# A transformer layer on one core: store queue, x tiles, operand order, buffer places and pool starts

## The chip, the cores and the metric

One core of a Trainium2 chip runs the kernel. The metric is device time in microseconds, the median of the runs shown. Engines: TensorE (PE, with weight loads as PEld), VectorE (DVE), ScalarE (ACT), GpSimd (POOL) and SyncE (SP), which issues most DMAs. SP, and ScalarE where it issues DMAs, take their instructions in order: an issue that waits holds up everything behind it on that engine.

## The reference

One layer on x of 2048 tokens by 1024 channels, float32, with a conditioning vector c:

```python
h = rms_norm(x, g_attn[l]) * (1.0 + scale_a) + shift_a
proj = h @ w_in[l]                      # q, k, v of 8 FoX heads and 8 stick-breaking heads, forget logits
mix = jnp.concatenate([head_rms_norm(o_fox, ...), head_rms_norm(o_sb, ...)], axis=-1)
x = x + gate_a * (mix @ w_out[l])
h = rms_norm(x, g_mlp[l]) * (1.0 + scale_m) + shift_m
u = causal_depthwise_conv(h @ w_up[l], conv_w[l], conv_b[l])     # 2 x 2752 columns, width 3
u_gate, u_val = jnp.split(u, 2, axis=-1)
x = x + gate_m * ((jax.nn.silu(u_gate) * u_val) @ w_down[l])
return rms_norm(x, g_final)
```

## The kernel before

Every matrix product keeps float32 accuracy by splitting each operand into a high part (fp32r) and the rest: `split` (L43 to L45) lets ScalarE write the high part and DVE or POOL subtract. Three matmuls (high·high, high·low, low·high) stand for one product.

The stages in order are the input projection with attention (to about 1.6 ms), the output projection, the up projection and the down projection.

**Output projection** (L623 to L738). Eight units `u` of 256 tokens. `make_mix` loads the attention output o and its scales r and splits the product into mix tiles, one unit ahead. `out_proj` takes two x1 tiles (`x1_tile`, L722: three buffers), loads x into each (L627, SP), computes 2 x 24 matmuls per tile (L632) and adds the result on DVE (L636); L637 stores the sum on SP. `finish_out` (L708) then scales the rows, transposes the two tiles on TensorE (L716), applies the modulation on ScalarE into hf_m tiles (L718, three buffers) and stores each to DRAM as h (L720, SP), 64 stores in all. An x1 tile is free again once the transposes of its unit are done.

**Up projection** (L741 to L926). Two half sequences `sblk` of 1024 tokens, each with 21 pairs of 128-column blocks and a rest of 64 columns. A Strassen-like scheme uses seven products over four index steps j instead of eight. `h_operands` loads two tiles xh of h per j and makes the operands: `oa` (the four blocks themselves, b12 replaced by b12 − b11) and `ob` (three differences), each split into two. j = 0's oa and ob lie in pool `hop0`, those of j = 1 to 3 in `hop1`. `w_operands` does the like with weight blocks (`ws`, `wu` in pool `wup`). The first pair of a half (`pair_first`, L823) runs all seven products of j = 0, then of j = 1, and so on, so that it can begin before all h is there; the other pairs (`pair`) run one product over all j. The first half needs only the tokens of units 0 to 3, so its work overlaps the end of the output projection. Then follow convolution (L871 to L881), SiLU, and a store of the product to DRAM as g (L903; L925 for the rest of 64).

**Down projection** (L928 to L999). For each of four blocks of 512 tokens, 22 steps k load a graw tile (L943) and a wdraw tile (L934), split both (`g` on ScalarE and POOL, `wd` on ScalarE and DVE, six buffers each) and run 24 matmuls (L966) into eight banks; L958 and L959 load gm and gf for the tail, where the residual add, the norm and two stores (L999, one on SP, one on ScalarE) follow.

**Pools.** SBUF is a stack from the left and one from the right. The constants lie at the bottom of the left one; `open_pool` opens a pool on either side, and a tile waits for the readers of the tiles whose bytes it takes. `hop0` and `wup` are on the right, `p2a`, `p2b`, `hop1`, `up` and `down` on the left. Left pools begin at byte 5440 and on, a multiple of 64; the right ones' tiles start 32 bytes off such a multiple. In the down projection, as it is before, every tile takes bytes of `hop1` and `up`.

The order of instructions on each engine is set when the program is built: the tile framework schedules them by a simulated timeline within the order that data and buffers leave free.

Of the kernel before, what the change touches and what calls it, by code (L numbers as in the profile page):

```python
# [16 lines left out]
P = 128  # L17
S = 2048
D = 1024
# [14 lines left out]
def kernel(ctx: ExitStack, tc: tile.TileContext, x, c, w_ada, b_ada, g_attn, w_in, b_fgate,  # L34
# [5 lines left out]
    def f(t):  # L40
        return t.bitcast(F32)
# [40 lines left out]
    epsc = const.tile([P, 1], F32, name="epsc")  # L82
    nc.vector.memset(epsc, EPS)

    cols = const.tile([P, P], F32, name="cols")
    conv = const.tile([P, 4, 2 * NFULL + 1], F32, name="conv")
    cs = const.tile([P, KT], F32, name="cs")
    mod_a = const.tile([P, 2, KT], F32, name="mod_a")
# [619 lines left out]
    def finish_out(u, xts):  # L708
        sl = slice(u % 4 * HT, (u % 4 + 1) * HT)
        r = rms_scale(p2b, xts, "m")  # L710
        for i, xt in enumerate(xts):
            nc.vector.tensor_scalar_mul(xt, xt, r[:, i:i + 1])
        for kt in range(KT):
            ps = bank(psd, "t", 2)
            for i, xt in enumerate(xts):
                nc.tensor.transpose(ps[:, i * P:(i + 1) * P], xt[:, kt * P:(kt + 1) * P], ident)  # L716
            hf = p2b.tile([P, HT], F32, name="hf_m", bufs=3)
            nc.scalar.activation(hf, ps[:, :HT], AF.Identity, scale=mod_m[:, 0, kt:kt + 1],  # L718
                                 bias=mod_m[:, 1, kt:kt + 1])
            nc.sync.dma_start(hms[u // 4][kt][:, sl], hf)  # L720

    def x1_tile():  # L722
        return p2b.tile([P, D], F32, name="x1", bufs=3)

    mixes = {}
    for u in range(NU):
# [26 lines left out]
    def h_operands(sblk, j):  # L753

        pool = ho if j == 0 else ho1
        xh = ho.tile([P, 2, SB], F32, name="xh", bufs=2)
        for i in range(2):
            nc.sync.dma_start(xh[:, i], hms[sblk][j + i * NK])
        b = pool.tile([P, 3, 2, TB], F32R, name=f"ob{j}")
        a = pool.tile([P, 4, 2, TB], F32R, name=f"oa{j}")  # L760
        tt = ho.tile([P, 2, TB], F32, name="tt", bufs=1)
        b11, b12 = xh[:, 0, 0:TB], xh[:, 0, TB:SB]
        b21, b22 = xh[:, 1, 0:TB], xh[:, 1, TB:SB]

        def put(hi, lo, s):
            split(hi, lo, s, nc.vector)

        put(a[:, 0, 0], a[:, 0, 1], b11)
        put(a[:, 1:3, 0], a[:, 1:3, 1], xh[:, 1].rearrange("p (a n) -> p a n", n=TB))
        nc.gpsimd.tensor_sub(tt[:, 0], b22, b12)  # L770
        nc.gpsimd.tensor_sub(b12, b12, b11)
        put(a[:, 3, 0], a[:, 3, 1], b12)
        nc.vector.tensor_sub(tt[:, 1], b22, b12)
        put(b[:, 0:2, 0], b[:, 0:2, 1], tt)
        nc.gpsimd.tensor_sub(b21, b21, tt[:, 1])
        put(b[:, 2, 0], b[:, 2, 1], b21)
        return [a[:, 0], b[:, 1], a[:, 1], a[:, 3], b[:, 0], a[:, 2], b[:, 2]], a

    def load_up(col_sets):
# [12 lines left out]
    def w_operands(ci):  # L792

        g, v = load_up([(ci * P, P)]), load_up([(DFF + ci * P, P)])
        a11, a12, a21, a22 = g[:, 0:NK], g[:, NK:KT], v[:, 0:NK], v[:, NK:KT]
        s3 = wp.tile([P, NK, P], F32, name="ws", bufs=4)
        s2 = wp.tile([P, NK, P], F32, name="ws", bufs=4)
        nc.gpsimd.tensor_sub(s3, a11, a21)
        nc.gpsimd.tensor_add(a21, a21, a22)
        nc.gpsimd.tensor_sub(s2, a21, a11)  # L800
        yield w_split(a11)
        yield w_split(s2)
        yield w_split(a12)
        nc.gpsimd.tensor_sub(a12, a12, s2)
        yield w_split(a21)
        yield w_split(s3)
        yield w_split(a12)
        yield w_split(a22)

    def product(b, w, o, j, first, last):  # L810
        for i, (p, q) in enumerate(((0, 0), (0, 1), (1, 0))):
            nc.tensor.matmul(b, w[:, p, j], o[:, q], start=first and i == 0, stop=last and i == 2,  # L812
                             skip_group_check=True)
# [9 lines left out]
    def pair_first(ws, yg, yv):  # L823

        banks = [bank(psd, "o", 4), bank(psd, "o", 4), bank(psd, "o", 4), bank(psd, "o", 4),
                 bank(psd, "t", 2), bank(psd, "t", 2), bank(psc, "bc", 2)]
        for j in range(NK):
            for b, w, o in zip(banks, ws, obs[j][0]):
                product(b, w, o, j, j == 0, j == NK - 1)
        b1, b6, b2, b5, b7, b3, b4 = banks  # L830
        p1, t, u3 = snap(), snap(), snap()
        nc.scalar.activation(p1, b1, AF.Copy)
        nc.vector.tensor_add(t, b6, p1)
        nc.vector.tensor_add(yg[:, T0], b2, p1)
        nc.vector.tensor_add(u3, b7, t)
        nc.vector.tensor_add(t, b5, t)
        nc.vector.tensor_add(yv[:, T1], b5, u3)
        nc.vector.tensor_add(yg[:, T1], b3, t)
        nc.vector.tensor_add(yv[:, T0], b4, u3)
# [85 lines left out]
        nc.sync.dma_start(gs[NFULL][sblk], sg[REST:P])  # L925
    close_pool("up", "hop1", "wup", "hop0")  # L926

    dp = open_pool("down")  # L928

    def load_down(k):  # L930
        n = P if k < NFULL else REST
        raw = dp.tile([P, D], F32, name="wdraw", bufs=3)
        for r in range(P // n):
            nc.sync.dma_start(raw[r * n:(r + 1) * n], w_down[k * P:k * P + n, :])  # L934
        w = dp.tile([P, 2, D], F32R, name="wd", bufs=6)
        split(w[:, 0], w[:, 1], raw, nc.vector)
        return w

    def load_g(k, tb):
        n = P if k < NFULL else REST  # L940
        raw = dp.tile([P, TB], F32, name="graw", bufs=3)
        for r in range(P // n):
            nc.sync.dma_start(raw[r * n:(r + 1) * n], gs[k][tb // 2][:, tb % 2 * TB:(tb % 2 + 1) * TB])  # L943
        g = dp.tile([P, 2, TB], F32R, name="g", bufs=6)
        if n == P:
            split(g[:, 0], g[:, 1], raw)
        else:
            nc.scalar.activation(g[:, 0], raw, AF.Copy)
            nc.vector.tensor_sub(g[REST:P, 0], raw[REST:P], f(g[REST:P, 0]))
        return g  # L950

    gm = dp.tile([P, D], F32, name="gm")
    gf = dp.tile([P, D], F32, name="gf")
    LAST = 4
    NKD = NFULL + 1
    for tb in range(NTB):
        if tb == 0:
            nc.sync.dma_start(gm, gate_m)  # L958
            nc.sync.dma_start(gf, g_final.rearrange("(o n) -> o n", o=1).to_broadcast([P, D]))  # L959
        banks = [[bank(psd, "o", 4) for _ in range(2)] for _ in range(2)]  # L960
        banks += [[bank(psd, "t", 2) for _ in range(2)], [bank(psc, "bc", 2) for _ in range(2)]]

        def step(k, g, w, t, n):
            seq = ((0, 0), (0, 1), (1, 0)) if k < NFULL else ((0, 0), (0, 1))
            for i, (a, b) in enumerate(seq):
                nc.tensor.matmul(banks[t][n], g[:, a, t * P:(t + 1) * P], w[:, b, n * TB:(n + 1) * TB],  # L966
                                 start=k == 0 and i == 0, stop=k == NKD - 1 and i == len(seq) - 1)

        tail = []
        for k in range(NKD):  # L970
            g, w = load_g(k, tb), load_down(k)
            if k >= NKD - LAST:
                tail.append((k, g, w))
                continue
            for t in range(4):
                for n in range(2):
                    step(k, g, w, t, n)
        for t in range(4):
            row = tb * 4 + t
            xt = dp.tile([P, D], F32, name="xo", bufs=4)  # L980
            nc.sync.dma_start(xt, x1s[row])
            ss = dp.tile([P, 2], F32, name="sl_f", bufs=4)
            r = dp.tile([P, 1], F32, name="r_f", bufs=4)
            for n in range(2):
                sl = slice(n * TB, (n + 1) * TB)
                for k, g, w in tail:
                    step(k, g, w, t, n)
                y = dp.tile([P, TB], F32, name="yo", bufs=3)
                nc.vector.tensor_mul(y, banks[t][n], gm[:, sl])
                nc.vector.tensor_add(xt[:, sl], xt[:, sl], y)  # L990
                junk = dp.tile([P, TB], BF16, name="junk_f", bufs=2)
                nc.scalar.activation(junk, xt[:, sl], AF.Square, accum_out=ss[:, n:n + 1])
            nc.vector.tensor_add(r, ss[:, 0:1], ss[:, 1:2])
            nc.scalar.activation(r, r, AF.Sqrt, bias=epsc, scale=1.0 / D)
            nc.vector.reciprocal(r, r)
            for n, q in enumerate((nc.sync, nc.scalar)):
                sl = slice(n * TB, (n + 1) * TB)
                nc.vector.scalar_tensor_tensor(xt[:, sl], xt[:, sl], r, gf[:, sl], ALU.mult, ALU.mult)
                q.dma_start(out[row * P:(row + 1) * P, sl], xt[:, sl])  # L999

    close_pool("down", "psd", "psc")

# [22 lines left out]
```

## Time and profile before

| | |
|---|---|
| median of 3 runs | 3206.13 us (3205.09 to 3209.88) |
| profiled execution | 3209.97 us, span 3207.9 us |
| TensorE busy | 3018.6 us, 94% of the span |
| DVE / ACT / POOL busy | 2178.5 / 1657.6 / 1230.3 us |
| output projection, units 1 to 7 | about 1641.8 to 1824 us |
| its end, with the first pair of the up projection | to 1870.5 us |
| change of half sequences | 2257.9 to 2301.3 us |
| last up matmul, first down matmul | 2708.95 us, 2726.28 us |

Times in views count from the start of the span. "PE ps_o L632 <- DVE x L636" says that the matmul of line 632, which writes tile ps_o, waited for DVE's instruction of line 636 on tile x. PEclk is the granted TensorE clock in parts of 2.4 GHz. A chain's "issue" is time in which an engine waited for nothing that is shown.

### The profile page before, as it was taken

How to read it: one execution, taken by the hardware profiler on the slowest of the kernel's cores; microseconds unless marked ns; L12 is line 12 of the kernel's file. 1: busy time of each engine (PE TensorE's matmuls, PEld its weight loads, DVE VectorE, ACT ScalarE, POOL GpSimd, SP SyncE). 2: the span in 40 equal slices, each digit the busy share in tenths (PEclk: the TensorE clock that was granted, in tenths of full speed). 3: DMA queues.
4: the chain of work that ended last, by engine and by line, in shares of the span. 5: the costliest groups of instructions: out<-in, count | busy, mean ns of one | idle time of the engine just before them, and what ended most of it. 6: DMA issues, size and time to landing. Idle time of an engine off the chain costs nothing. (4 is left out here: it accounts for less than half of the span.)

```text
span 3207.9 us, 46681 instructions
## 1 busy us (share of the span) xinstructions
PE 3018.6 (94%) x16190; PEld 2526.4 (79%) x16190; DVE 2178.5 (68%) x3335; ACT 1657.6 (52%) x3033; POOL 1230.3 (38%) x1399
## 2 busy tenths in 40 slices
PE   7899898999899999999988899999899997999999
PEld 5778787878778888888866678888688886888887
DVE  6787888978867765557733477777887786354353
ACT  5666676656656665566633344444544443333332
POOL 2554455656542232240132234444544442322221
PEclk8999999999999999999998899999999999999999
DMA  8547542556355876593466332222232222664652
GB/s 262 177 153 255 149 142 53 169 187 180 105 171 167 278 245 200 177 331 100 164 201 214 138 103 83 82 82 80 76 92 83 82 79 78 221 200 149 199 200 86
DMA packets 292940, 496.53 MB, mean 155 GB/s; under 512 B 29448, under 2 KB 177664, under 8 KB 291680
## 3 DMA queue, kind: packets, MB, share of 16 engines
q1 hardware_dynamic: 290288, 489.32, 47.7%
q10 hardware_dynamic: 2416, 4.23, 0.3%
q8 instruction: 128, 2.10, 0.3%
q14 instruction: 108, 0.88, 0.1%
HBM read 352.61 MB, written 90.51 MB: 138 GB/s over the span
## 5 line engine op out<-in xcount | busy, mean ns | idle before, releaser
L812 PE MATMUL ps_o<-oa,wu 128*128 128x512 f32 x2088 | 514.2, 397 | 7.1 <-ACT oa L44 3.9
L812 PEld LDWEIGHTS ps_o<-oa,wu 128*128 128x128 f32 x2088 | 392.9, 189 | 105.9 <-ACT oa L44 5.3
L405 PE MATMUL ps_pv<-at,V 128*128 128x256 f32 x2304 | 412.1, 297 | 32.5 <-DVE at L401 19.5
L401 DVE TENSOR_TENSOR at<-ps_pt,at 128x512 fp32r<-128x512 f32 (+1 forms) x576 | 363.4, 651 | 111.1 <-ACT at L400 108.4
L287 PE MATMUL ps_pj<-hp,w_qk 128*128 128x512 f32 x1512 | 417.0, 407 | 11.2 <-POOL hp L45 3.4
L400 ACT ACTIVATE at<-ps_pt 128x512 fp32r<-128x512 f32 (+1 forms) x576 | 315.7, 577 | 215.3 <-PE ps_pt L396 173.8
L426 DVE TENSOR_TENSOR_SCAN r<-r 128x513 f32<-128x513 f32 (+2 forms) x320 | 383.6, 1213 | 38.6 <-ACT r L419 29.2
L427 POOL TENSOR_TENSOR a<-a,r 128x512 f32<-128x512 f32 (+3 forms) x240 | 280.4, 1171 | 308.3 <-DVE r L426 178.9
L405 PEld LDWEIGHTS ps_pv<-at,V 128*128 128x128 f32 x2304 | 334.0, 192 | 69.8 <-DVE at L401 33.1
L287 PEld LDWEIGHTS ps_pj<-hp,w_qk 128*128 128x128 f32 x1512 | 275.5, 192 | 65.8 <-POOL hp L45 4.5
L45 DVE TENSOR_TENSOR wd<-wdraw,wd 128x1024 fp32r<-128x1024 f32 x88 | 125.9, 1430 | 247.5 <-ACT wd L44 247.5
L384 PE MATMUL ps_qk<-K,Q 128*128 128x512 f32 (+2 forms) x640 | 268.4, 419 | 13.9 <-ACT a L420 6.4
L966 PE MATMUL ps_o<-wd,g 128*128 128x512 f32 x1040 | 249.9, 390 | 17.3 <-ACT wd L44 17.3
L45 POOL TENSOR_TENSOR g<-graw,g 128x512 fp32r<-128x512 f32 x84 | 119.2, 1422 | 356.4 <-ACT g L44 337.6
L44 ACT ACTIVATE wu<-wuraw 128x512 fp32r<-128x512 f32 x214 | 133.9, 628 | 225.8 <-PE ps_o L812 196.2
L812 PE MATMUL ps_t<-ob,wu 128*128 128x512 f32 x984 | 249.7, 399 | 0.0
L326 PE MATMUL ps_pj<-w_v,hp 128*128 128x256 f32 (+1 forms) x1536 | 241.9, 294 | 3.4 <-DVE q L45 1.1
L966 PEld LDWEIGHTS ps_o<-wd,g 128*128 128x128 f32 x1040 | 196.0, 189 | 58.5 <-ACT wd L44 17.8
L385 PE MATMUL ps_qk<-K,Q 128*128 128x512 f32 (+2 forms) x640 | 237.7, 372 | 0.0
L326 PEld LDWEIGHTS ps_pj<-w_v,hp 128*128 128x128 f32 x1536 | 213.0, 194 | 13.1 <-DVE q L296 1.4
L812 PEld LDWEIGHTS ps_t<-ob,wu 128*128 128x128 f32 x984 | 186.7, 190 | 45.5 <-ACT hf_m L718 0.2
L419 ACT ACTIVATE r<-ps_qk 128x512 f32<-128x512 f32 (+2 forms) x320 | 172.7, 540 | 59.8 <-PE ps_qk L385 32.4
(221 smaller groups left out, 5726.4 us busy)
## 6 DMA issues: line engine op xcount, KB each, us to landing
hp<-hs SPq DMA_DIRECT2D x224, 512.0 KB
wuraw<-in_w_up_dram SPq DMA_DIRECT2D x84, 512.0 KB
wdraw<-in_w_down_dram SPq DMA_DIRECT2D x84, 512.0 KB
Q<-q SPq DMA_DIRECT2D x128, 256.0 KB
g<-u SPq DMA_DIRECT2D x42, 512.0 KB
graw<-g SPq DMA_DIRECT2D x84, 256.0 KB
hs<-hp SPq DMA_DIRECT2D x32, 512.0 KB
K<-q SPq DMA_DIRECT2D x128, 128.0 KB
```

Of the source, the lines that this page charges most:

```text
L45: (lo_engine or nc.gpsimd).tensor_sub(lo, src, f(hi))
L287: nc.tensor.matmul(acc, w[kt][:, a, n], h[:, bb], start=kt == 0 and i == 0, stop=kt == KT - 1 and i == 2)
L326: nc.tensor.matmul(av[:, t * width:(t + 1) * width], hts[kt][:, a, tok], w[1][kt][:, bb, 0:width], start=kt == 0 and m == 0, stop=kt == KT ...
L384: nc.tensor.matmul(b[:, :cw], Q[:, hl, 0, qcols], K[:, hl, :cw], start=True, stop=False)
L385: nc.tensor.matmul(b[:, :cw], Q[:, hl, 1, qcols], K[:, hl, :cw], start=False, stop=not last)
L400: nc.scalar.activation(at[:, 0, lo:], b[:, lo:], AF.Copy)
L401: nc.vector.tensor_sub(at[:, 1, lo:], b[:, lo:], f(at[:, 0, lo:]))
L405: nc.tensor.matmul(o[:, 0:2 * P], V[kt // 4][:, kt % 4, hl, :], rhs, start=first and kk == 0 and w == 0, stop=last and kk == 1 and w == 1)
L426: nc.vector.tensor_tensor_scan(rev, rev, rev, 1.0, ALU.mult, ALU.bypass)
L427: (nc.vector if (ch + qi) % 4 == 0 else nc.gpsimd).tensor_mul(a[:, :need], a[:, :need], r[:, 1:need + 1])
L812: nc.tensor.matmul(b, w[:, p, j], o[:, q], start=first and i == 0, stop=last and i == 2, skip_group_check=True)
L966: nc.tensor.matmul(banks[t][n], g[:, a, t * P:(t + 1) * P], w[:, b, n * TB:(n + 1) * TB], start=k == 0 and i == 0, stop=k == NKD - 1 and i ...
```

## The change

- The tile `cols` in the constant pool grows by 40 floats, 160 bytes for each partition; every pool on the left side begins 160 bytes later (5440 becomes 5600), the right ones stay.
- `finish_out`: two hf_m buffers instead of three, and the store of h is issued by ScalarE. `x1_tile`: four buffers instead of three.
- `h_operands`: the differences and `ob` are made first, then `oa`; the difference that POOL made in place in b21 is made by DVE into a tile t4 from the buffers of tag `ws`, which are three instead of four. `pair_first` issues the products of each j in the order 1, 4, 6 (operands from ob), 0, 2, 5, 3.
- The down projection's g, wdraw, graw (two buffers instead of three) and wd lie in a pool on the right side, on the bytes of `hop0` and `wup`; the loads of a k step are issued weights first. gm, gf, xo, yo (four buffers instead of three), junk and the row sums lie in a new pool `end` on the left.

```diff
-    cols = const.tile([P, P], F32, name="cols")
+    cols = const.tile([P, P + 40], F32, name="cols")
...
-            hf = p2b.tile([P, HT], F32, name="hf_m", bufs=3)
+            hf = p2b.tile([P, HT], F32, name="hf_m", bufs=2)
...
-            nc.sync.dma_start(hms[u // 4][kt][:, sl], hf)
+            nc.scalar.dma_start(hms[u // 4][kt][:, sl], hf)
...
-        return p2b.tile([P, D], F32, name="x1", bufs=3)
+        return p2b.tile([P, D], F32, name="x1", bufs=4)
...
+        t4 = wp.tile([P, TB], F32, name="t4", tag="ws", bufs=3)
...
+        nc.gpsimd.tensor_sub(tt[:, 0], b22, b12)
+        nc.gpsimd.tensor_sub(b12, b12, b11)
+        nc.vector.tensor_sub(tt[:, 1], b22, b12)
+        nc.vector.tensor_sub(t4, b21, tt[:, 1])
+        put(b[:, 0:2, 0], b[:, 0:2, 1], tt)
+        put(b[:, 2, 0], b[:, 2, 1], t4)
         put(a[:, 0, 0], a[:, 0, 1], b11)
         put(a[:, 1:3, 0], a[:, 1:3, 1], xh[:, 1].rearrange("p (a n) -> p a n", n=TB))
-        nc.gpsimd.tensor_sub(tt[:, 0], b22, b12)
-        nc.gpsimd.tensor_sub(b12, b12, b11)
         put(a[:, 3, 0], a[:, 3, 1], b12)
-        nc.vector.tensor_sub(tt[:, 1], b22, b12)
-        put(b[:, 0:2, 0], b[:, 0:2, 1], tt)
-        nc.gpsimd.tensor_sub(b21, b21, tt[:, 1])
-        put(b[:, 2, 0], b[:, 2, 1], b21)
...
-            for b, w, o in zip(banks, ws, obs[j][0]):
-                product(b, w, o, j, j == 0, j == NK - 1)
+            for s in (1, 4, 6, 0, 2, 5, 3):
+                product(banks[s], ws[s], obs[j][0][s], j, j == 0, j == NK - 1)
...
-    dp = open_pool("down")
+    dp = open_pool("down", side="right")
+    def load(k, tb):
         n = P if k < NFULL else REST
+        g = dp.tile([P, 2, TB], F32R, name="g", bufs=6)
+        wraw = dp.tile([P, D], F32, name="wdraw", bufs=3)
+        graw = dp.tile([P, TB], F32, name="graw", bufs=2)
+        w = dp.tile([P, 2, D], F32R, name="wd", bufs=6)
         for r in range(P // n):
+            nc.sync.dma_start(wraw[r * n:(r + 1) * n], w_down[k * P:k * P + n, :])
+            nc.sync.dma_start(graw[r * n:(r + 1) * n], gs[k][tb // 2][:, tb % 2 * TB:(tb % 2 + 1) * TB])
+        split(w[:, 0], w[:, 1], wraw, nc.vector)
...
+    de = open_pool("end")
+    gm = de.tile([P, D], F32, name="gm")
...
-                y = dp.tile([P, TB], F32, name="yo", bufs=3)
+                y = de.tile([P, TB], F32, name="yo", bufs=4)
```

## Rows read from the trace of the kernel before

**Rows 1.** The page, totals: engine, busy us, share of the span, instructions.

```profile
PE 3018.6 (94%) x16190; PEld 2526.4 (79%) x16190; DVE 2178.5 (68%) x3335; ACT 1657.6 (52%) x3033; POOL 1230.3 (38%) x1399
```

**Rows 2.** Windows by stage: stretch, length, busy us per engine, PEclk, DMA share, GB/s.

```profile
1641.80:1824.20 182.40, 155.32 (x665) 124.48 (x666) 60.28 (x100) 62.59 (x132) 46.89 (x53) 0.91 0.57 189
1824.20:1870.50 46.30, 35.34 (x135) 25.32 (x134) 29.35 (x35) 22.17 (x38) 19.15 (x17) 0.85 0.49 153
1870.50:2257.90 387.40, 387.40 (x1662) 311.94 (x1661) 299.49 (x337) 171.18 (x238) 170.93 (x158) 1.00 0.26 81
2257.90:2301.30 43.40, 32.94 (x112) 21.96 (x110) 36.53 (x35) 22.70 (x30) 28.18 (x16) 0.84 0.29 91
...
2726.30:3195.00 468.70, 468.70 (x2060) 388.03 (x2061) 196.06 (x206) 162.74 (x247) 117.98 (x83) 1.00 0.54 178
```

**Rows 3.** Windows: sum of five stretches at granted clock 0.50, output projection.

```profile
sum 34.10, PE 23.56 PEld 18.00 DVE 17.69 ACT 13.83 POOL 3.55; mean PE 4.71 PEld 3.60 DVE 3.54 ACT 2.77 POOL 0.71
```

**Rows 4.** Windows: sum of two stretches at 0.50, end of that stage.

```profile
sum 13.60, PE 9.58 PEld 7.06 DVE 3.81 ACT 4.47 POOL 1.06; mean PE 4.79 PEld 3.53 DVE 1.90 ACT 2.23 POOL 0.53
```

**Rows 5.** Windows at 0.50: change of half sequences, start of the down projection.

```profile
2279.70:2293.30 13.60, 10.16 (x20) 5.58 (x19) 12.03 (x10) 5.36 (x7) 8.97 (x6) 0.50 0.41 119
2713.20:2730.20 17.00, 3.92 (x9) 3.14 (x10) 4.16 (x4) 5.67 (x7) 4.15 (x3) 0.50 0.77 266
```

**Rows 6.** Waits of PE, output projection: us in total, times, longest.

```profile
PE ps_o L632 <- DVE x L636: 22.7, 7, 8.7
PE ps_t L716 <- ACT hf_m L718: 8.6, 6, 3.1
```

**Rows 7.** Chain of waits, one pause of the output projection: start, us, what.

```profile
1742.61 5.92 DMA x<-in_x_dram
...
1752.12 6.67 DMA xh<-hm
```

**Rows 8.** Waits of SP's queue, output projection.

```profile
SPq L720 <- ACT hf_m L718: 37.9, 16, 8.4
```

**Rows 9.** Chain of waits, end of the output projection.

```profile
1832.01 4.86 DMA x<-in_x_dram
...
1847.67 2.24 DMA hm<-hf_m
...
1850.37 4.08 DMA hm<-hf_m
```

**Rows 10.** Line 999, its issues on ScalarE's queue: duration ns min/median/max.

```profile
L999 ACTq DMA_DIRECT2D out_dram<-xo x16: 338/339/380, 2837.3 to 3204.7; - x16
```

**Rows 11.** Timeline of PE, change of half sequences: in brackets idle before, releaser.

```profile
2279.49 0.67 PE L812 MATMUL ps_bc<-ob,wu 128*128 128x512 f32 x1 [4.93 <-ACT ob L44]
...
2284.61 1.95 PE L812 MATMUL ps_o<-oa,wu 128*128 128x512 f32 x3 [2.78 <-ACT oa L44]
```

**Rows 12.** Groups, change of half sequences: busy us, mean ns, idle before.

```profile
L771 POOL TENSOR_TENSOR xh<-xh 128x512 f32<-128x512 f32 x3 | 5.3, 1778 | 0.2
...
L775 POOL TENSOR_TENSOR xh<-xh,tt 128x512 f32<-128x512 f32 x3 | 4.5, 1508 | 2.7 <-DVE tt L773 2.7
...
L773 DVE TENSOR_TENSOR tt<-xh 128x512 f32<-128x512 f32 x3 | 2.1, 684 | 1.2 <-POOL xh L771 1.2
...
L799 POOL TENSOR_TENSOR wuraw<-wuraw 128x512 f32<-128x512 f32 x1 | 1.3, 1261 | 0.1
```

**Rows 13.** Chain of waits, start of the down projection.

```profile
2701.24 7.71 PE ps_o L812 x33
...
2716.05 0.48 SPq L925
...
2718.39 6.70 DMA wdraw<-in_w_down_dram
...
2725.17 1.07 ACT wd L44
```

**Rows 14.** The page's groups: the input projection's matmuls.

```profile
L287 PE MATMUL ps_pj<-hp,w_qk 128*128 128x512 f32 x1512 | 417.0, 407 | 11.2 <-POOL hp L45 3.4
```

More of the change, by code (lines that the diff above doesn't have):

```diff
@@ L795, in w_operands @@
         a11, a12, a21, a22 = g[:, 0:NK], g[:, NK:KT], v[:, 0:NK], v[:, NK:KT]
-        s3 = wp.tile([P, NK, P], F32, name="ws", bufs=4)
-        s2 = wp.tile([P, NK, P], F32, name="ws", bufs=4)
+        s3 = wp.tile([P, NK, P], F32, name="ws", tag="ws", bufs=3)
+        s2 = wp.tile([P, NK, P], F32, name="ws", tag="ws", bufs=3)
         nc.gpsimd.tensor_sub(s3, a11, a21)
@@ L926 @@
     close_pool("up", "hop1", "wup", "hop0")
-    dp = open_pool("down")
-    def load_down(k):
+    dp = open_pool("down", side="right")
+    def load(k, tb):
         n = P if k < NFULL else REST
-        raw = dp.tile([P, D], F32, name="wdraw", bufs=3)
+        g = dp.tile([P, 2, TB], F32R, name="g", bufs=6)
+        wraw = dp.tile([P, D], F32, name="wdraw", bufs=3)
+        graw = dp.tile([P, TB], F32, name="graw", bufs=2)
+        w = dp.tile([P, 2, D], F32R, name="wd", bufs=6)
         for r in range(P // n):
[L934 to L944, printed above, removed]
+            nc.sync.dma_start(wraw[r * n:(r + 1) * n], w_down[k * P:k * P + n, :])
+            nc.sync.dma_start(graw[r * n:(r + 1) * n], gs[k][tb // 2][:, tb % 2 * TB:(tb % 2 + 1) * TB])
+        split(w[:, 0], w[:, 1], wraw, nc.vector)
         if n == P:
-            split(g[:, 0], g[:, 1], raw)
+            split(g[:, 0], g[:, 1], graw)
         else:
[L948 to L953, printed above, removed]
+            nc.scalar.activation(g[:, 0], graw, AF.Copy)
+            nc.vector.tensor_sub(g[REST:P, 0], graw[REST:P], f(g[REST:P, 0]))
+        return g, w
+    de = open_pool("end")
+    gm = de.tile([P, D], F32, name="gm")
+    gf = de.tile([P, D], F32, name="gf")
     LAST = 4
@@ L970 @@
         for k in range(NKD):
-            g, w = load_g(k, tb), load_down(k)
+            g, w = load(k, tb)
             if k >= NKD - LAST:
@@ L979 @@
             row = tb * 4 + t
-            xt = dp.tile([P, D], F32, name="xo", bufs=4)
+            xt = de.tile([P, D], F32, name="xo", bufs=4)
             nc.sync.dma_start(xt, x1s[row])
-            ss = dp.tile([P, 2], F32, name="sl_f", bufs=4)
-            r = dp.tile([P, 1], F32, name="r_f", bufs=4)
+            ss = de.tile([P, 2], F32, name="sl_f", bufs=4)
+            r = de.tile([P, 1], F32, name="r_f", bufs=4)
             for n in range(2):
@@ L987 @@
                     step(k, g, w, t, n)
-                y = dp.tile([P, TB], F32, name="yo", bufs=3)
+                y = de.tile([P, TB], F32, name="yo", bufs=4)
                 nc.vector.tensor_mul(y, banks[t][n], gm[:, sl])
                 nc.vector.tensor_add(xt[:, sl], xt[:, sl], y)
-                junk = dp.tile([P, TB], BF16, name="junk_f", bufs=2)
+                junk = de.tile([P, TB], BF16, name="junk_f", bufs=2)
                 nc.scalar.activation(junk, xt[:, sl], AF.Square, accum_out=ss[:, n:n + 1])
@@ L999 @@
                 q.dma_start(out[row * P:(row + 1) * P, sl], xt[:, sl])
-    close_pool("down", "psd", "psc")
+    close_pool("end", "down", "psd", "psc")
 _INS = ['x', 'c', 'w_ada', 'b_ada', 'g_attn', 'w_in', 'b_fgate', 'g_out_fox', 'g_out_sb', 'w_out', 'g_mlp', 'w_up',
```

## The prediction

> **What bounds the kernel now.** I read the engine totals first: TensorE is busy for 94% of the span [rows 1]. The reader is to see there that only the missing 6%, and the pace of the matmuls themselves, can give anything. Then the windows by stage [rows 2]: a whole half of the up projection and the down projection are TensorE from edge to edge (387.40 of 387.40 us, 468.70 of 468.70, at a granted clock of 1.00). The seams are not: in the output projection TensorE works 155.32 of 182.40 us, at its end 35.34 of 46.30, at the change of half sequences 32.94 of 43.40, and between the last up matmul, which ends at 2701.24 + 7.71 = 2708.95, and the split that lets the first of the down projection go, which ends at 2726.24, it has nothing [rows 13]. The idle time of the four is 27.1 + 11.0 + 10.5 + 17.3 = 65.9 us. Third, the clock: stretches that follow such pauses run at 0.50, the lower of the two levels (1.2 GHz). In five of the projection TensorE is busy for 23.56 us in all [rows 3], in two at its end for 9.58 [rows 4], in the two at the other seams for 10.16 and 3.92 [rows 5]; at twice the clock half of each would do, so 11.8 + 4.8 + 5.1 + 2.0 = 23.7 us are lost. All that waits and clock can return is 89.6 us.
>
> **Output projection (fourth x1 tile, stores of h on ScalarE's queue).** The waits of TensorE name DVE's residual add, 22.7 us in 7 waits, longest 8.7 [rows 6]. The chain shows why [rows 7]: the x load is issued at 1742.61, in the middle of the pause, and lands 5.92 us later; only then can the add run. The load comes late for two reasons. With three tiles and two per unit, a unit's second tile is one that the unit before still transposes. And SP, in order, stood at L720 behind hf_m for 37.9 us in 16 waits [rows 8]. A fourth tile lets both loads of a unit go while the unit before computes; moving L720 takes SP's waits away. So 22.7 us go, less what is late next: the unit's first x load still has to pass SP's loads of r and o, and I leave 2.7 us. That is −20.0. What TensorE loses to hf_m (8.6 us in 6, [rows 6]) I reduce by 2 only, since two hf_m buffers instead of three make that wait harder. The half clock of the five stretches cost 11.8 us [rows 3]; 10 of it goes with the pauses.
>
> At the end of the stage the last unit's second x load is issued at 1832.01 and takes 4.86 us; later in the chain stand two landings of h, 2.24 and 4.08 us [rows 9]. The load moves ahead by a unit, the landings stay: of 11.0 us idle and 4.8 of clock [rows 4] I take 6. The sum is −20 − 2 − 10 − 6 = −38; bounds −46 (all of the 22.7 and 16.6, 6.7 at the end) and −22 (L632's waits alone).
>
> The moved store costs ScalarE one issue each, 0.34 us by the ACT-queue row of L999 [rows 10], 64 × 0.34 = 21.8 us on an engine that is busy 62.59 + 22.17 of 228.7 us [rows 2]: I cost it at nothing. Behind a store of h on ScalarE stand the next hf_m and the splits of mix; for the latter DVE waits, a unit ahead of TensorE.
>
> The Trainium skill speaks against this edit: "DMA: Bandwidth & Descriptors", section "Issuing engines are not separate DMA queues", says that transfers started by several engines share the same 16 DMA engines, and only the sequencer's time is saved. By that rule the 64 issues alone come off SP. By it the part is worth what 64 issues of SP cost, and those hide; −38 would be near −20, what the fourth tile alone may do. The trace says that SP loses more than issues at L720: 37.9 us of waits [rows 8], with the DMA engines at a share of 0.57 [rows 2].
>
> **Change of half sequences (b operands first, t4 on DVE).** TensorE stands longest for an ob split, 4.93 us, then for an oa split, 2.78 [rows 11]. pair_first consumes seven products in step with each j, so every j needs all of its operands soon, and DVE is busy 36.53 of 43.40 us [rows 2]. The edit moves the subtraction of L775 (POOL, 1.51 us, 3 in the window) to DVE at the price of L773's 0.68 us [rows 12]: four of them add 2.7 us to the engine that is busiest, and take a hop POOL–DVE out of each ob chain. The b products issued first need ob, which comes first. What is late next is DVE's own sum, so at most 43.4 − 36.5 − 2.7 = 4 us can go from idle time, and about 2 of the 5.1 us of clock: −6. Bounds: −13 (most of 10.5 idle and 5.1 clock) and +5 (2.7 us on DVE plus the half clock stretched by as much).
>
> The Trainium skill's page "SBUF — State Buffer", section "Who interferes with whom", says that a DVE instruction with two inputs in SBUF and a GpSimd instruction that reads SBUF hold each other up, and that TensorE never waits on anyone. The first half agrees with the trace: L771 takes 1.78 us beside DVE's splits, L799, of the same shape, 1.26 [rows 12]. By it the move gives POOL back more than its share; DVE stays the bound either way. By the second half only the operands' own places would be left to explain the two paces of TensorE below.
>
> **Down projection's start (right-hand pool, weights first).** The chain [rows 13]: after the last up matmul DVE and ScalarE finish the last columns; SP issues their store at 2716.05, then by the code's order gm, gf, graw, and wdraw, which starts at 2718.39 and takes 6.70 us; ScalarE's split takes 1.07. In the new place the first weights and g lie on bytes whose readers end at the last j = 0 products, about nine matmuls (2.1 us) before the end, instead of on bytes that the u tiles hold until 2716. The loads can go once SP has passed the store of the last full column block, which I put at about 2708, beside the last matmuls (an estimate). Then 4.86 us (the x load of [rows 9], alike in size) to 6.70, and 1.07 for the split: TensorE starts at 2714 to 2716, so 10 to 12 us of 17.3 go, and 2 of clock: −14 if loads are a little ahead of that store. Bounds −19.3 (all) and −9.
>
> gm, gf, xo and the fourth yo buffer serve only the end of a token block of 468.7 / 4 = 117 us [rows 2]: nothing. Two graw instead of three: a g split can be late by up to six k steps (six g buffers), each 24 matmuls of 0.2275 us = 5.5 us; nothing, and one such step per block if that cover is gone.
>
> **The 160 bytes.** They shift every pool of the left side; those on the right stay. Matmul pace differs by stage: 387.40 / 1662 = 233.1 ns in the up projection and 468.70 / 2060 = 227.5 in the down projection [rows 2], same shape, same clock. In the up projection three of four moving operands lie on the left and the weights on the right; before, left pools start at a multiple of 64 bytes and right pools 32 bytes off. In the down projection both operands lie on the left. One reading: unlike starts cost 5.6 to 6.6 ns, and alike ones, which the pad makes everywhere, don't: 3072 × 6.6 = −20 us. The other: a start 32 bytes off costs, and the down projection, which moves to the right, pays 2080 × 6.6 = +14, and the input and output projections, left-side on both operands, up to (1512 + 768) × 6.6 = 15 more [rows 14]. Both fit the two rows. I weigh them two to one, as the second asks that the weights' start counts by itself (three of four moving operands of up start on a multiple of 64, and the stage is slow all the same): (2 × −20 + 14) / 3 = −8.7, and −7 with something for neither; both ends are kept.
>
> **Sum.** −38 − 6 − 14 − 7 = −65 us. The profiled execution took 3209.97 us (span 3207.9), 3.8 more than the median of 3206.13; the stages differ in waits and not in that offset, so I subtract from the median: 3141.
>
> **Rivals.**
> - R1, alike starts pay in full: −58 − 20 gives 3128. For it: the two paces; against: no row shows one stage at both offsets.
> - R2, the 32-byte start itself costs: −58 + 14 gives 3162, with the projections' 15 it is 3177. For it: the same two rows; against: it has to be the weights alone, as said.
> - R3, the down projection's loads stay where they are, since SP, in order, has them behind the store that waits until 2716.05: without the 14, and of the pad 7, 3155. For it: [rows 13] has them there.
> - R4, ScalarE is caught by its own stores (slower than before). With two hf_m buffers each activation waits for the landing of the store two before it. A pair of hf_m then takes 1.11 + 0.34 + landing, four pairs a unit. At the 6.67 us that xh takes in [rows 7] this is 8.1 × 4 = 32.5 us a unit against 182.4 / 7 = 26.1 now: +45 over seven units, and 3206 + 45 − 27 = 3224. It decides from landings of 26.1 / 4 − 1.45 = 5.1 us on. Against: the landings in the chain are 2.24 and 4.08 us [rows 9].
> - R5, the moved work only changes what waits, within 0.2% (6.4 us, about what a measurement of this kernel can tell).
>
> **How the numbers follow.** Forecast 0.48, own range 3130 to 3152; R1 0.2; R2 0.1; R3 0.14; R4 0.06; R5 0.02. The range of 3112 to 3172 takes in R1 with larger gains at the seams (their bounds are 8, 7 and 5 us better), R3 and two thirds of R2, and leaves out R4 and R5. Faster: 0.92; same 0.02; slower 0.06.
>
> **What would show it.** L632's waits for L636 under 5 us and L720 on the ACT queue; stretches at 0.50 in the projection fewer than three; the window of half change 35 to 40 us; first L966 within 3 to 7 us of the last L812; the pace in the up projection 226 to 228 (R1) or 233, in the down projection 227 or 233 (R2). It would be wrong if hf_m's waits for landings grew past 20 us, or if the matmuls of both stages changed pace together.

## The result and the profile after

The changed kernel takes 3151.14 us in the median (3145.07 to 3151.99, 4 runs), the kernel before beside it 3205.61 (3202.72 to 3209.88): a ratio of 0.9825, 95% interval 0.9808 to 0.9842, or −54.5 us. Forecast was 3141, −65. The profiled execution of after is the fastest of its four, that of before the slowest of its own, so the two spans differ by 64.6 us, some 10 us more than the medians do; sizes below come from medians where there are any.

The page of after, totals, against [rows 1]: TensorE is busy for 28.5 us less, though it runs the same 16190 matmuls.

```profile
PE 2990.1 (95%) x16190; PEld 2521.1 (80%) x16190; DVE 2158.8 (69%) x3343; ACT 1652.0 (53%) x3033; POOL 1215.3 (39%) x1391
```

The windows by stage of after (columns as in [rows 2]): output projection from 1598, its end, first half of the up projection, change of half sequences, second half, gap, down projection.

```profile
1598.00:1792.60 194.60, 179.19 (x831) 143.66 (x831) 74.69 (x130) 78.21 (x165) 54.07 (x63) 0.98 0.66 218
1792.60:1824.80 32.20, 25.25 (x92) 16.36 (x90) 28.32 (x28) 19.52 (x33) 13.96 (x9) 0.89 0.44 139
1824.80:2205.00 380.20, 379.08 (x1664) 311.94 (x1665) 300.78 (x341) 171.07 (x241) 163.19 (x162) 1.00 0.29 85
2205.00:2262.00 57.00, 47.47 (x181) 35.16 (x180) 54.09 (x58) 28.80 (x40) 23.74 (x19) 0.94 0.25 79
...
2653.30:2662.10 8.80, 0.02 (x1) 0.00 (x0) 5.00 (x5) 3.87 (x4) 0.00 (x0) 0.79 1.02 343
2662.10:3130.00 467.90, 467.88 (x2058) 387.36 (x2059) 183.00 (x205) 163.28 (x247) 141.36 (x84) 1.00 0.53 179
```

Three things moved and one didn't. The projection runs at a mean granted clock of 0.98; the like stretch of before, with the up projection's first matmuls in it, had 0.92 over 226.4 us:

```profile
1598.00:1824.40 226.40, 192.44 (x851) 153.67 (x850) 79.67 (x133) 81.13 (x169) 60.73 (x68) 0.92 0.56 184
```

In the up projection 379.08 us hold 1664 matmuls, 227.8 ns each against 233.1 in [rows 2]. The gap before the down projection is 8.80 us instead of 17.3. At the change of halves TensorE still idles, for 9.5 of 57.0 us.

TensorE's waits in the projection of after, against [rows 6]: those for the residual add (L636) are gone; those for hf_m are not (before, from 1598 on, they were 11.9 us in 8).

```profile
PE ps_t L716 <- ACT hf_m L718: 9.9, 8, 2.5
PE ps_o L813 <- DVE oa L45: 4.1, 5, 1.3
PE ps_o L632 <- ACT mix L44: 2.9, 3, 1.1
```

### The profile page after: what moved, and what is told of

The parts are those of the page before. It is cut to its first block, busy times and chain, and to the rows that moved or that the text cites. A ratio compares the mean times of both kernels' runs of the same rounds, so it can differ in the third digit from the quotient of the medians.

```text
span 3143.3 us, 46642 instructions
## 1 busy us (share of the span) xinstructions
PE 2990.1 (95%) x16190; PEld 2521.1 (80%) x16190; DVE 2158.8 (69%) x3343; ACT 1652.0 (53%) x3033; POOL 1215.3 (39%) x1391
## 4 chain that ended last, share of the span: by engine, by line
PE 57%; DVE 13%; DMA 12%; POOL 7%; issue 6%; ACT 4%; SPq 1%; ACTq 0%; POOLq 0%; DVEq 0%
PE ps_pj L287 8%; PE ps_o L963 8%; PE ps_pv L405 6%; PE ps_o L813 6%; PE ps_pt L396 5%; PE ps_pj L326 5%; PE ps_t L963 4%; PE ps_bc L963 4%; DMA wuraw<-in_w_up_dram 3%; PE ps_qk L384 3%; PE ps_qk L385 3%; DVE r L426 2%; DVE wu L45 2%; PE ps_t L813 2%; DMA Q<-q 2%
## 5 line engine op out<-in xcount | busy, mean ns | idle before, releaser
L813 PE MATMUL ps_o<-oa,wu 128*128 128x512 f32 x2088 | 503.3, 392 | 12.6 <-DVE oa L45 7.5
L287 PE MATMUL ps_pj<-hp,w_qk 128*128 128x512 f32 x1512 | 414.1, 405 | 11.9 <-POOL hp L45 3.4
L45 DVE TENSOR_TENSOR wd<-wdraw,wd 128x1024 fp32r<-128x1024 f32 x88 | 112.2, 1275 | 260.9 <-ACT wd L44 260.8
L45 POOL TENSOR_TENSOR g<-graw,g 128x512 fp32r<-128x512 f32 x84 | 141.4, 1685 | 325.9 <-ACT g L44 325.8
L813 PE MATMUL ps_t<-ob,wu 128*128 128x512 f32 x984 | 241.6, 390 | 0.0
L396 PE MATMUL ps_pt<-ident,a 128*128 128x128 f32 x1088 | 185.6, 280 | 21.7 <-POOL a L427 13.2
```

The lines of the kernel that those rows point to most:

```text
L45: (lo_engine or nc.gpsimd).tensor_sub(lo, src, f(hi))
L287: nc.tensor.matmul(acc, w[kt][:, a, n], h[:, bb], start=kt == 0 and i == 0, stop=kt == KT - 1 and i == 2)
L396: nc.tensor.transpose(b[:, i * P:(i + 1) * P], blk(kts[kk], qi), ident)
```

## The experiments

Each has the changed kernel ("after") or the kernel before as its base, and differs by the edit shown. Medians are of four to ten runs, with the kernel before run beside them on the same chip, unless a run is called single.

**The fourth tile or the queue of the stores.** First the tile alone is taken back:

```diff
-        return p2b.tile([P, D], F32, name="x1", bufs=4)
+        return p2b.tile([P, D], F32, name="x1", bufs=3)
```

> The changed kernel with three x1 tiles again; the stores of h stay on ScalarE's queue. Theory 1 (the fourth tile takes away TensorE's waits for the residual add): the waits of L632 for L636 are back at 15 to 23 us with stretches at half clock behind them, 3151 + 28 = 3179 us. Rival (SP's place behind hf_m made the x loads late, and the move of the stores cured it): the waits stay under 5 us, 3151 to 3157 us.

Measured: 3189.97 us, ratio 0.9949 (0.9935 to 0.9964), 38.8 us more than after. Its waits of TensorE are as they were before, though the stores are on ScalarE's queue, and its clock from 1598 to 1822 is 0.90:

```profile
PE ps_o L632 <- DVE x L636: 23.5, 7, 7.6
PE ps_t L716 <- ACT hf_m L718: 13.2, 5, 4.5
```

```profile
1598.00:1822.00 224.00, 189.79 (x814) 151.79 (x813) 78.37 (x130) 79.51 (x165) 55.02 (x64) 0.90 0.56 185
```

SP, no longer held at L720, now stands at the x load itself (L627), until the transposes free a tile; in after it stands there for 1.0 us:

```profile
SPq L627 <- PE ps_t L716: 33.9, 4, 22.0
```

Then the queue alone is taken back:

```diff
-            nc.scalar.dma_start(hms[u // 4][kt][:, sl], hf)
+            nc.sync.dma_start(hms[u // 4][kt][:, sl], hf)
```

> The changed kernel with the stores of h on SP's queue again (two hf_m buffers and four x1 tiles stay). Theory 1 (the fourth tile does it): SP stands at L720 again, but the x loads are a unit early and TensorE does not wait: 3151 to 3156 us. Rival (the queue does it): the waits of L632 come back, 3165 to 3179 us.

Measured: 3151.30 us, ratio 0.9831 (0.9816 to 0.9846): no difference from after. SP stands at L720 again, here in SP's own waits from 1598 to 1800, and TensorE waits for the residual add once, for 2.9 us:

```profile
SPq L720 <- ACT hf_m L718: 18.6, 18, 4.1
```

```profile
PE ps_t L716 <- ACT hf_m L718: 9.6, 9, 2.9
PE ps_o L813 <- DVE oa L45: 3.7, 3, 2.7
PE ps_o L632 <- DVE x L636: 2.9, 1, 2.9
```

With four tiles an x load that is issued some microseconds late is still early. Without the fourth it can't be early, whatever queue is free, since its buffer is not: that is the 33.9 us. So the tile is worth the 39 us and the queue nothing that these runs show. With three tiles it is worth nothing either: the other parts, as measured below, bring the kernel before to 3206.55 − 17.3 − 6.3 + 5.7 = 3188.7 us, and three tiles with the moved queue took 3189.97. SP's 37.9 us of [rows 8] were not what TensorE waited for.

**The 160 bytes.** Taken out of after, and put alone into before:

```diff
-    cols = const.tile([P, P + 40], F32, name="cols")
+    cols = const.tile([P, P], F32, name="cols")
```

> The changed kernel with the 160 bytes taken out again (cols back to 128 columns). Left pools start at a multiple of 64 bytes again, right pools 32 bytes off. Theory 1 (operands that start alike modulo 64 are fast): the up projection is back at 233 ns a matmul, the down projection stays at 227, in all about 3151 + 20 = 3171 us. Theory 2 (the pad did nothing, the pace of the up projection changed through the new operand order or pools): up stays at 227, 3151 us.

> The kernel before with the 160 bytes alone. Theory 1: up projection at 227 ns, the others as they were, 3206 - 20 = 3186 us. Theory 2: 3206 us, up at 233. If the wait pattern of the output projection moves with it, the sum differs, but the median start-to-start spacing of L812 tells.

Measured: 3167.09 us without it (0.9878, 0.9859 to 0.9897), 16.0 more than after; 3187.07 with it alone (0.9932, 0.9915 to 0.9949), 17.3 less than before beside it (22 by the ratio). The pad is worth much the same in either kernel. To see what it acts on I took, of each kernel, 250 us of the up projection's second half, in which TensorE is never or hardly idle (a few records may be missing); the pace is the length over the count behind PE's busy time. Before, 233.0 ns:

```profile
2399.00:2649.00 250.00, 250.00 (x1073) 201.32 (x1072) 195.70 (x217) 110.46 (x153) 114.08 (x77) 1.00 0.27 82
```

After without the pad, 233.0, and before with the pad alone, 226.9:

```profile
2358.00:2608.00 250.00, 250.00 (x1073) 201.33 (x1072) 199.76 (x219) 109.38 (x154) 114.91 (x77) 1.00 0.27 83
```

```profile
2377.00:2627.00 250.00, 249.93 (x1102) 206.16 (x1101) 195.03 (x222) 109.81 (x156) 111.25 (x80) 1.00 0.28 83
```

So it is the pad. After itself keeps 227.3 ns (1099 matmuls in 249.80 us). The line that multiplies (L812) runs 3624 such matmuls in the trace of before, not 3072 as the prediction's working has it, and 3624 × (233.0 − 226.9) ns = 22.1 us is what the pace is worth if all of them keep it; the interval of the pad's ratio on before, 16 to 27 us, takes that in. What about the pad does it? Three single runs move the stacks further. The right side by 32 bytes, with the pad of 160 (the tile comes first on the right stack):

```diff
+    shim = open_pool("shim", side="right")
+    shim.tile([P, 8], F32, name="shim")
     sb = open_pool("sb", side="right")
```

> The changed kernel with the right-hand side shifted by 32 bytes (a tile of 8 floats at its base), so that left pools start 32 bytes off a multiple of 64 and right pools at a multiple: up projection with weights at a multiple of 64 and three of four moving operands 32 off, the reverse of before. Theory 1 (alike or not): up at 233, about 3171 us. Theory 2a (only weights that start 32 bytes off cost, in company of a moving operand that does not): up at 227, 3151 us.

The left side of after by 32 bytes instead of 160, then of before by 416:

```diff
-    cols = const.tile([P, P + 40], F32, name="cols")
+    cols = const.tile([P, P + 8], F32, name="cols")
```

> The changed kernel with a pad of 32 bytes in place of 160: left pools start at 5472, alike with the right modulo 64 (32) but not modulo 512 (352 against 480). Theory 1 (modulo 64 decides): up at 227, about 3151 us. Theory 1b (a longer period, 128 to 512 bytes, decides): up at 233, about 3171 us.

```diff
-    cols = const.tile([P, P], F32, name="cols")
+    cols = const.tile([P, P + 104], F32, name="cols")
```

> The kernel before with a pad of 416 bytes: left pools start at 5856, 224 modulo 512, right ones at 480, 256 bytes apart. Theory 1b (the distance between the two operands' starts modulo 512 decides, near is fast): up at 231 to 233 ns. Theory 1c (the distance modulo 256 decides, which the 231 ns at a distance of 128 allows): up at 227 ns.

The rows of the three in this order, 232.3, 231.1 and 226.9 ns (their times, 3166.45, 3170.07 and 3199.63 us, are of one execution each and not read here; the last section says why):

```profile
2364.00:2614.00 250.00, 250.00 (x1076) 201.62 (x1076) 200.89 (x219) 109.43 (x155) 115.89 (x77) 1.00 0.27 83
```

```profile
2368.00:2618.00 250.00, 250.00 (x1082) 203.21 (x1081) 206.50 (x219) 108.91 (x154) 118.01 (x77) 1.00 0.26 83
```

```profile
2388.00:2638.00 250.00, 249.93 (x1102) 206.11 (x1101) 194.86 (x222) 109.63 (x156) 111.53 (x80) 1.00 0.27 83
```

The distance between the left and the right starts is 160 bytes in before (at 320 and 480 modulo 512), 0 in after, 32 in the first single run, 128 in the second, 256 in the third. Distances 0 and 256 give 226.9, 128 gives 231.1, 160 and 32 give 233.0 and 232.3. "Alike modulo 64" falls with the second run (both 32 off, and slow), "modulo 512" with the third. What is left is the distance between the two sides modulo 256, as far as five distances show it. The first run also turns the roles round, weights at a multiple of 64 and moving operands 32 off, and is slow: it is not the weights' start by itself. In both fast layouts the two sides stand at 224 modulo 256, so the up projection alone can't tell the distance from that place. The down projection can: its operands lie on one side, and it runs 1766 or 1767 matmuls in 400 us, 226.4 to 226.5 ns, with both at 64 modulo 256 (before), at 224 (after) or at 192 (first single run). Whether a distance of 64 would be slow was not tried.

One observation doesn't fit so simply. The products of j = 0 have both operands on the right, at distance 0, in every run. Taken from start to start, they still need 232 ns in before, 231 in the first single run and 230 in the second; in the fast layouts it is 227. Mostly they come three at a time, between products of another j. Where the first pair of a half runs nine or more of them in a row, without a pause and at full clock, they come down to 226 and 227 ns, after five to nine matmuls: in the first single run, from 1797.83 us on, 226, 236, 228, 233, 231, then 226, 227, 227, 226, 227, 227. So the distance of a matmul's own operands is not all that sets its pace, and those just before it seem to count too; how, no run here shows.

**The operands at the change of halves.** The new order, t4 and three ws buffers alone on before, and the old order (with three ws buffers) on after. The edit is the part of the change's diff between `t4` and the loop over (1, 4, 6, 0, 2, 5, 3), forth and back; of the second, in short:

```diff
-        nc.vector.tensor_sub(t4, b21, tt[:, 1])
-        put(b[:, 2, 0], b[:, 2, 1], t4)
+        nc.gpsimd.tensor_sub(b21, b21, tt[:, 1])
+        put(b[:, 2, 0], b[:, 2, 1], b21)
...
-            for s in (1, 4, 6, 0, 2, 5, 3):
-                product(banks[s], ws[s], obs[j][0][s], j, j == 0, j == NK - 1)
+            for b, w, o in zip(banks, ws, obs[j][0]):
+                product(b, w, o, j, j == 0, j == NK - 1)
```

> The kernel before with the new order of the operands, DVE's t4, three ws buffers and the new order of the products in pair_first, nothing else. Theory 1 (DVE's and ScalarE's sum of work bounds the change of halves, the order only moves the waits): idle time of TensorE from the end of the first half's rest to 2330 us stays at 10 to 12 us, the whole within 3 us of 3205. Rival (the forecast): idle there falls by 4 us and the half clock by 2, 3199 us.

> The changed kernel with the old making of the operands (oa first, POOL's difference in b21, no t4) and the old order of the products in pair_first; three ws buffers as after the change. Theory 1 (the new order is worth nothing at the change of halves and disturbs the projection's end, as its 6 us on the kernel before show): 3145 to 3151 us. Rival (only together with the early x loads does the new order pay): 3155 us and more, with more idle time of TensorE between 1790 and 1830 us.

Measured: 3212.28 us on before (1.0021, 1.0006 to 1.0035), so 5.7 us slower; 3143.46 without it on after (0.9808, 0.9788 to 0.9829 against 0.9825), 7.7 us faster; the two intervals overlap, but no run of the one (3141.64 to 3144.80) is among those of the other (3145.07 to 3151.99). At the change itself it does a little, as 85 us from the end of the first half on show, before and then with the new order:

```profile
2257.00:2342.00 85.00, 74.16 (x287) 54.94 (x286) 74.92 (x78) 43.47 (x60) 46.56 (x31) 0.92 0.26 78
```

```profile
2270.00:2355.00 85.00, 75.65 (x293) 56.50 (x292) 77.95 (x84) 42.52 (x60) 36.61 (x26) 0.94 0.28 84
```

Six matmuls more, 1.5 us of TensorE's time. DVE is busy for 3.0 us more, about the 2.7 that four new subtractions cost, and POOL for 10 less. TensorE's waits have changed their names. Before, in the same stretch, and then with the new order:

```profile
PE ps_bc L812 <- ACT ob L44: 5.2, 2, 4.9
PE ps_o L812 <- ACT oa L44: 2.8, 1, 2.8
PE ps_o L812 <- DVE oa L45: 1.5, 1, 1.5
```

```profile
PE ps_o L813 <- ACT oa L44: 3.5, 2, 2.8
PE ps_o L813 <- DVE oa L45: 3.2, 2, 2.4
PE ps_o L813 <- ACT wu L44: 1.5, 2, 1.2
```

The loss lies where the first half's operands are made, in the output projection and its end. Of after, the stretch from the last matmul of the projection to the last transposes, and some us on, is in the second row of the windows above: 32.2 us, 25.25 of them busy. With the old order it is

```profile
1788.90:1813.00 24.10, 19.27 (x76) 13.10 (x75) 24.10 (x23) 17.24 (x29) 11.85 (x7) 0.93 0.41 134
```

The two hold different numbers of matmuls (92 and 76), so what compares is TensorE's idle time, 6.9 us and 4.8. The same matmuls in more traces say it better. From the last of L632 to the 151st of the up projection it is 49.9 to 52.7 us in six traces with the new order and four x tiles, and 47.2 and 47.4 in the two with the old order. On the kernel before it is 56.1 and with the new order 58.1, and there units 1 to 7 of the output projection (L632) take 218.8 us instead of 212.0. DVE is busy in 24.10 of 24.10 us of the stretch shown, so an extra subtraction on it has no free time to go to; but that the extra work on DVE is what delays the stage is argued, since no run adds or removes t4 alone.

**The down projection's start.** Its pools and loads alone on before (the part of the change's diff from `dp` on):

```diff
-    dp = open_pool("down")
+    dp = open_pool("down", side="right")
...
+    de = open_pool("end")
```

> The kernel before with the down projection's pools and loads of the changed kernel, nothing else. Theory 1 (the gap ends with the first weights' load, which SP issues behind the store of the last full column block, gm and gf): gap of 8 to 9 us instead of 17.3, 3205 - 9 = 3196 us, pace of the down projection 227 ns. Rival 1 (the right side's 32 bytes cost): 233 ns, +14. Rival 2 (the gap is smaller only thanks to the other parts): gap of 14 us or more.

Measured: 3200.22 us (0.9981, 0.9971 to 0.9991), 6.3 less than before, with a gap of 2717.35 − 2709.01 = 8.3 us (17.3 before) and an unchanged pace: 3190.58 − 2717.35 = 473.2 us from the first to the last matmul, against 473.6 before. What fills the gap is in the chain, here of after:

```profile
2651.26 1.24 DVE u L903
...
2652.51 0.32 SPq L904
...
2652.93 0.38 SPq L955
...
2653.35 0.78 SPq L956
...
2654.23 6.24 DMA wdraw<-in_w_down_dram
...
2660.49 1.06 ACT wd L44
2661.55 0.53 ACT g L44
```

SP waits for DVE's last product of the last full block (L903), stores it, issues gm and gf, and only then the first weights, whose 6.24 us are all in the gap. By the layout of the pools the first weights' bytes are those of a weight buffer that the rest block no longer uses; it is the queue that keeps them waiting. Which part of the edit, the place or the order of the loads, brought them ahead of the rest block's store was not taken apart. So the next kernel loads them early, into 6 KB that lie free between the two stacks, and gm and gf late:

```diff
+    early = open_pool("early")
+    wraw0 = early.tile([P, D], F32, name="wdraw0")
+    graw0 = early.tile([P, TB], F32, name="graw0")
...
+            if sblk and ci == 18:
+                nc.sync.dma_start(wraw0, w_down[0:P, :])
+                nc.sync.dma_start(graw0, gs[0][0][:, 0:TB])
...
+            if tb == 0 and k == 8:
+                nc.sync.dma_start(gm, gate_m)
```

> The changed kernel with the first weights and g of the down projection loaded, three column blocks before the end of the up projection, into 6 KB that lie free between the two stacks, and gm and gf loaded at the ninth step. Theory 1 (the gap of 8.8 us is the landing of wdraw behind the last full block's store, gm and gf): gap 1 to 3 us, 3151 - 7 = 3144 us. Rival (ScalarE's order, which has the split behind the last copies of the up projection, sets the gap, or the second step's load comes late in its place): 5 us of gap stay in all, 3148 us.

Measured: 3140.21 us (0.9799, 0.9780 to 0.9817), 10.9 less than after by the medians and 8 by the ratios, around the gap of 8.8 that it was to close; the intervals just overlap, the runs themselves don't. The timeline of TensorE (columns as in [rows 11]) has no gap before the first matmul of the down projection, and one of 0.50 us at its second step, whose weights still come behind the store:

```profile
2650.78 4.47 PE L813 MATMUL ps_o<-oa,wu 128*128 128x512 f32 x19
2655.09 1.44 PE L969 MATMUL ps_o<-wd,g 128*128 128x512 f32 x4
...
2661.59 1.21 PE L969 MATMUL ps_o<-wd,g 128*128 128x512 f32 x4 [0.50 <-ACT g L44]
```

**Both last steps together**, the old order of the operands and the early loads:

> Both last steps together: the changed kernel with the old making of the operands and order of products (three ws buffers) and the first loads of the down projection early, gm and gf at the ninth step. Theory (the two parts act at different places, the end of the output projection and the start of the down projection, and add): 3151 - 7.7 - 10.9 = 3132 us, gap before the down projection 0 to 1 us. Rival (one of them was spread between runs of other stages): 3137 to 3143 us.

Measured: 3135.46 us (0.9776, 0.9762 to 0.9789; 3129.13 to 3141.49): the interval lies under that of after, and it beats both kernels, by 70.5 and 15.7 us. That is between theory and rival (3132, 3137 to 3143). Against the early loads alone it is 4.8 less, with overlapping intervals, so that the old order pays on top is likely and not shown.

## Why the prediction was right, and where its steps were not

The direction and the range held, the narrower range of 3130 to 3152 just so; the sum of −65 was 10 too large. It came that near by luck in part, because errors in both signs met.

- **Output projection, −38.** The fourth tile alone is worth −38.8, so the size was right, and the signs named for it came: no wait for the residual add is left, and one stretch at 0.50 within units 1 to 7 instead of five. The working named two causes of the late load and took both as needed; one was enough. The Trainium skill's sentence that was weighed there ("DMA: Bandwidth & Descriptors", "Issuing engines are not separate DMA queues") had the edit of the queue right: moving the stores saves nothing but issue time, and that was hidden. What the text drew from the rule was wrong, namely that the rest would then be near −20: the tile does the whole.
- **hf_m, 2 of these 38.** Over the whole stage TensorE's waits for hf_m went from 11.9 to 9.9 us, 8 each: as reckoned, and with the stores back on SP they are 9.6, so it is not the queue either. R4's mechanism is there, in ScalarE's own waits for landings in after, but far from its price:

```profile
ACT hf_m L718 <- DMA hm<-hf_m: 16.8, 9, 3.9
```

  Nine waits for 64 tiles, 16.8 us in all on an engine that has the time, where R4 needed one at nearly every pair.
- **Change of halves, −6.** This step failed. The gain was read off idle time of TensorE with DVE busy for 36.5 of 43.4 us; the order moved the waits from ob to oa and gave 1.5 us back. The step did not ask what the same code does for the first half, whose operands are made beside the projection: there the edit costs more than it gives here, 6 to 8 us in all by the two runs.
- **Down projection's start, −14.** Right in kind, mis-sized: the gap shrank by 9.0 us, to 8.3, and the time by 6.3, with an interval of 3 to 9; the sign named, a gap of 3 to 7, did not come. The text put the load at about 2708 (with this part alone it is at 2709.54) and reckoned 4.86 to 6.70 for it; but gm and gf stand ahead of it, two issues of 0.4 and 0.8 us, and the landing took 6.16 to 6.24 us with the DMA engines at a share of 1.02. The "little ahead of that store" on which −14 rested did not happen, since SP issues in order and had the store, gm and gf first. R3, no gain at all, was wrong.
- **The 160 bytes, −7.** The step weighed two readings two to one; the first was right, with −16 to −17, and R1 was in this term the forecast to take. The working's 3072 matmuls stand in no row: with the 3624 that the trace has, its −20 would have been −24. R2's +14 did not come: on the right side, 32 bytes off, the down projection kept its pace. The "two conditions" of the step were mended by the runs: not the start modulo 64 of one operand, but the distance between the two sides, with the open end that j = 0 leaves.

The measured parts add up: −38.8 (tile) − 16.0 (pad) − 6.3 (down) + 5.7 (order) + 0 (queue) = −55.4, beside −54.5. Each term is known to some 3 to 5 us only, so it is chance that they meet within 1; that no large part is missing they do show.

## What to carry to other kernels

A queue that stands in a wait for 38 us has not been shown to cost anything until something on the bounding engine is shown to wait for it: ask first whether the buffer behind the late load was free at all. Where the bounding engine has no gap, look at its pace, the same instruction at 233 ns in one stage and 227 in another; where the operands lie was worth 16 to 17 us here, for 160 bytes. A load that opens a stage belongs into bytes that are free early and, on an in-order queue, ahead of the store that ends the stage before.

## What the runs showed of the hardware

- The pace of the up projection's 128x512 matmuls at a granted clock of 1.00 depends on where the left and the right pools, moving operands and weights, start against each other within a partition: 226.9 ns at distances of 0 and 256 bytes, 231.1 at 128, 232.3 at 32, 233.0 at 160. By the Trainium skill ("SBUF — State Buffer", "Who interferes with whom") TensorE waits on no other engine, and these runs agree in so far as the pace moved with the operands alone, at much the same busy time of DVE and POOL.
- The same instructions up to the attention ended at different times in different executions: the first matmul of the output projection starts at 1530.73 us in after with the old order and at 1536.92 in both last steps together, which differ in the first loads of the down projection alone. Between after and the last of the three single runs it is 10 us (1530.83 and 1540.87). That is as much as neighbouring distances differ by, so single runs were read by their pace and not by their time.
